# A bidirectional RWKV scan under dense products on one core: product order tied to the emission model, transposes for token rows, merged DMA issues

## The chip, the cores and the metric

One core of a Trainium2 chip. The metric is the device time of one execution in microseconds (us), from a profile of that core; lower is better. "Before" is the kernel as it stands, and the change is one edit of it.

## What is computed

One layer of a backbone over 1024 latent and 128 context tokens, D = 1024, all in float32. The part that the change touches is the token mixer:

```
h = rmsnorm(x) * (1 + scale) + shift
z = h @ w_in                       # r, k, v, low-rank decay/iclr/gate inputs, conv inputs, merge gates
for d in (forward, backward):      # 16 heads of 64
    s = s * w_t + (s @ a_t) b_t^T + v_t k_t^T ;  y_t = s @ r_t
o_a = (groupnorm(y_f + y_b) + bonus) * g
merged = g_a * (o_a @ w_pa) + g_b * (o_b @ w_pb)
x = x + gate * (merged @ w_o)      # then rmsnorm, up projection, 3-tap convolution, silu, down projection
```

The outputs are both token streams and the final scan states of the context.

## The kernel before, in words

**Dense products.** The T = 1152 token columns are cut into three stretches of 384 (`TH`). Every weight block and every input is split into a rounded high part and a rest (`split_w`, L212), so that one 128x128x384 product is three fp32r matmuls: psd<-h,whi twice and psd<-h,wlo once. A job is 128 output channels: 8 k x 3 stretches x 3 = 72 matmuls, plus evacuations on ACT or DVE. w_in has 67 jobs (4824 matmuls) and w_pb 8 (576); these 5400 run beside the scan. Then come w_pa and w_o (576 each) and the feed-forward part.

**The scan** (class `Scan`, `start` L1019) is cut into 36 items: 4 groups of four heads times 9 positions (8 latent chunks of 2 x 64 tokens for each direction, and one context item). `prep` (L1106) computes per channel pair p and stretch the decayed r, k, kk and b rows from the loads krk<-ks, kks, rs (L1114) and llo<-lo (`lora_in`, L1183) and stores them to DRAM in FA and FB (L1178). Then each item goes through: `features` (L1190: loads BK<-fb, E and O<-fa); the 64 gram products gpb, gpk (L1223) with their masks on DVE (G, E, O); `to_blocks` and `chain_load` (Dd<-G, Dm<-Dd through DRAM); `chain` (L1301), 31 x 2 dependent DVE operations Xt<-X,Dm and X<-X,Xt, whose result goes through DRAM back into G (Xd<-X on ACT's queue, G<-Xd on SP's); `merge` (L1325), a DVE transpose RSt<-G (L1330) and two rounds of 16 small products mps; bps (L1244), the token rows of b and k as products of 64x64 blocks with the identity; `vfill` (L1252), which loads v rows into Wt; and `scan` (L1356), twice per item (c = 0, 1): px<-Wt,E/O and py, copy SX, px<-SX,G, copies into Wt (ACT, and DVE COPY at L1387), px<-Wt,BT and py<-G,Wt, then two DVE adds that make the next state in Wt. `finish` (L1429) normalises the outputs (products fps) and stores them to oa, from which w_pa's inputs are loaded (x<-oa).

**Order.** Each of these is a generator, a stream. `drive` (L172) runs a model clock: `mm` adds a product's price to it, `Stream.use` books time on DVE, ACT and POOL. Between two dense matmuls, `step_streams` (L151) advances every stream whose own model time has come; what a stream emits gets a scheduling priority 20000 places ahead (`later`, `AHEAD`). The framework's scheduler then places each instruction on its engine's queue by priority and its own estimate; every engine runs its queue in order, and so a product that was put early is waited for with all dense matmuls behind it.

Of the kernel before, what the change touches and what calls it, by code (L numbers as in the profile page):

```python
# [15 lines left out]
P = 128  # L16
D = 1024
# [59 lines left out]
class Kern:  # L77
    def __init__(self, tc, ins, outs):
        self.tc, self.nc = tc, tc.nc
        self.ins, self.outs = ins, outs  # L80
        self.clk = Clock()
        self.streams = []
        self.events = set()
        self.split, self.split_next = "V", "G"


    def mm(self, out, lhsT, rhs, start, stop, cost):
        self.clk.now += cost
        return self.nc.tensor.matmul(out, lhsT=lhsT, rhs=rhs, start=start, stop=stop)  # L89

# [7 lines left out]
    def transp(self, out, in_, ident, cost=60):  # L98
        self.clk.now += cost
        return self.nc.tensor.transpose(out, in_, ident)  # L100

# [49 lines left out]
    def step_streams(self):  # L151
        while True:
            for s in list(self.streams):
                if s.t > self.clk.now:
                    continue
                if s.cond is not None and not s.cond():
                    continue
                if s.gate is not None and max(self.clk.backlog("V"), self.clk.backlog("A")) > s.gate:
                    continue
                s.cond = None  # L160
                try:
                    with self.later(-AHEAD - s.ahead):
                        r = next(s.gen)
                    if callable(r):
                        s.cond = r
                except StopIteration:
                    self.streams.remove(s)
                break
            else:
                return  # L170
# [171 lines left out]
def build(tc, ins, outs, dbg=None):  # L342
# [4 lines left out]
    with es:  # L347
# [9 lines left out]
        dt_ = lambda name, shape=(P, T): dr.tile(list(shape), F32, name=name, tag=name)  # L357
        RS = [dt_(f"rs{m}") for m in range(8)]
        KS = [dt_(f"ks{m}") for m in range(8)]
        KKS = [dt_(f"kks{m}") for m in range(8)]  # L360
        VS = [dt_(f"vs{m}") for m in range(8)]
        LO = [dt_(f"lo{m}") for m in range(4)]
# [3 lines left out]
        VT = [dt_(f"vt{d}", (T, D)) for d in range(2)]  # L366
        GS = [dt_(f"gs{m}") for m in range(8)]
# [142 lines left out]
        with ExitStack() as ea:  # L510
# [16 lines left out]
            K.sc = Scan(K, const, apool, par, pc, mask, ident, bones, x0, hw0, hka, oka,  # L527
                        dict(RS=RS, KS=KS, KKS=KKS, VS=VS, LO=LO, GS=GS, OA=OA, FA=FA, FB=FB, BS=BS, VT=VT))
            hx = lambda k: (H[k][0], H[k][1])
# [9 lines left out]
            def lora_evac(base, func):  # L539
                def ev(s, th, ps):  # L540
                    sl = slice(th * TH, th * TH + TH)
                    z = st.tile([P, TH], F32, name="lz", tag="st")
                    K.act(s, z, ps, func)
                    hi = st.tile([P, TH], F32R, name="lh", tag="st")
                    lo = st.tile([P, TH], F32R, name="ll", tag="st")
                    K.act(s, hi, z, AF.Copy)
                    K.tt(s, lo, z, hi.bitcast(F32), ALU.subtract)
                    for d in range(2):
                        K.dma(LO[base + d][0:64, sl], hi[64 * d:64 * d + 64, :].bitcast(F32), "lo")
                        K.dma(LO[base + d][64:128, sl], lo[64 * d:64 * d + 64, :].bitcast(F32), "lo")  # L550
                return ev

            job(T_WD, lora_evac(0, AF.Tanh))
            job(T_AD, lora_evac(2, AF.Copy))

# [9 lines left out]
            def g_evac(s, m, th, ps):  # L565
                z = st.tile([P, TH], F32, name="gz", tag="st")
                K.act(s, z, ps, AF.Copy)
                K.dma(GS[m][:, th * TH:th * TH + TH], z, "gs")
# [13 lines left out]
            def v_evac(m):  # L582

                def ev(s, th, ps):
# [8 lines left out]
                    def post(s2):  # L593
                        t0, ms = th * TH, slice(m * P, m * P + P)
                        for d, zd in enumerate((z, zr)):
                            yield
                            pv = K.psd.tile([P, 512], F32, name="vps", tag="psd")
                            for j in range(3):
                                K.transp(pv[:, j * P:j * P + P], zd[:, j * P:j * P + P], ident, cost=110)
                            s2.t = clk.now  # L600
                            zt = st.tile([P, 3, P], F32, name="vt", tag="st")
                            K.act(s2, zt, pv[:, :TH].rearrange("p (j f) -> p j f", f=P), AF.Copy)
                            for a, b, _ in latctx(th):
                                r0 = t0 + a if d == 0 or t0 + a >= TL else TL - t0 - b
                                K.dma(VT[d][r0:r0 + b - a, ms].rearrange("(j t) f -> t j f", t=P),
                                      zt[:, a // P:b // P], "vt")
                        K.events.add(("v", m, th))
# [76 lines left out]

            rkv(0)
            rkv(1)
            job(T_GD, gd_evac)
            gjobs()
# [295 lines left out]
class Scan:  # L984
# [4 lines left out]
    def __init__(self, K, const, apool, par, pc, mask, ident, bones, x0, hw0, hka, oka, dr):  # L989
# [25 lines left out]
        self.W = self.one.tile([P, 2, 4, 2, C], F32, name="Wt", tag="Wt")  # L1015
        self.y, self.PC = {}, {}
        self.NY = 4

    def start(self):  # L1019
# [4 lines left out]
        def prep_all(s):  # L1024
            yield lambda: ("kk", 0, 0) in ev and ("r", 0, 0) in ev
            self.lora_in(0, 0)
            for p in range(NPAIR):
                yield lambda: ("kk", p, 0) in ev and ("r", p, 0) in ev
                yield from self.lora_w(s, p)
                for th in (0, 2, 1):  # L1030
                    yield lambda: ("kk", p, th) in ev and ("r", p, th) in ev
                    yield from self.prep(s, p, th)
                    ev.add(("prep", p, th))

        def ready(i, what):
            pp, n = self.items[i]
            ths = {n // 3, (7 - n) // 3} if n < 8 else {2}
            return all((what, 2 * pp + q, th) in ev for q in range(2) for th in ths)

        def prep2_all(s):  # L1040
            for i, (pp, n) in enumerate(self.items):
                yield lambda: ready(i, "prep") and (i < 3 or ("scan", i - 3) in ev)
                self.features(s, i, pp, n)
                s.t = K.clk.now + 2500
                yield
# [60 lines left out]
    def prep(self, s, p, th):  # L1106
# [6 lines left out]
        krk = self.one.tile([P, 3, TH], F32, name="krk", tag="krk")  # L1113
        for j, src in enumerate((dr["KS"], dr["KKS"], dr["RS"])):  # L1114
            K.dma(krk[:, j, :], src[p][:, t0:t0 + TH], "ld")
        if pp not in self.PC:
# [5 lines left out]
        for d in range(2):  # L1122
# [52 lines left out]
            for a, b in segs:  # L1175
                g0 = t0 + a if d == 0 or t0 + a >= TL else TL - t0 - b
                K.act(s, PC[:, q, d, g0 // C:(g0 + b - a) // C], e65[:, a // C:b // C, C], AF.Copy)
                for dst, src in (("FA", FAo), ("FB", B)):  # L1178
                    K.dma(dr[dst][pp][:, q, d, 2 * g0:2 * (g0 + b - a)],
                          src[:, a // C:b // C].rearrange("p c a t -> p (c a t)"), "fa")  # L1180
            yield

    def lora_in(self, th, d):  # L1183

        llo = self.one.tile([P, 2, TH], F32R, name="llo", tag="llo")
        for w in range(2):
            self.K.dma(llo[:, w, :].bitcast(F32), self.dr["LO"][2 * w + d][:, th * TH:th * TH + TH], "llo")
        self.llo = llo, self.K.clk.now + 4000
# [19 lines left out]
    def prep2(self, s, i, pp, n):  # L1208
# [5 lines left out]
        for q in range(2):  # L1214
# [4 lines left out]
            for e in range(4 * q, 4 * q + 4):  # L1219
                for ps, a in ((gb, 1), (gk, 0)):  # L1220
                    for h in range(2):
                        o = HS[h if a else 1 - h]
                        calls.append(lambda ps=ps, a=a, h=h, e=e, o=o: K.mm(  # L1223
                            ps[o, e - 4 * q, :], BK[HS[h], e, a, :], (E, O)[h][HS[h], e, :], True, True, 85))
            K.group(calls)
# [12 lines left out]
        for x in range(4):  # L1238
            for c in range(2):
# [12 lines left out]
    def vfill(self, s, i, pp, n):  # L1252
# [5 lines left out]
        for c in range(2):  # L1258
# [8 lines left out]
            ch = (2 * n + c if n < 8 else c) * C  # L1267
            for d in range(2):
                rows = self.dr["VT"][d][base + ch:base + ch + C, 256 * pp:256 * pp + 256]
                rows = rows.rearrange("t (q h f) -> t q h f", q=2, h=2)  # L1270
                for h in range(2):
                    K.dma(Wt[64 - 64 * h:128 - 64 * h, h, d::2, c, :], rows[:, :, h, :], "v")
            if c == 0 and n == 8:
# [155 lines left out]
    def finish(self, s, pp, key):  # L1429
# [7 lines left out]
        for q in range(2):  # L1437
# [9 lines left out]
            v, g, b = flat(v3), flat(g3), flat(b3)  # L1447
            s.t = K.clk.now + 2500
            yield
# [83 lines left out]
```

## Time and profile before

| | us |
|---|---|
| three runs, median (lowest to highest) | 3005.72 (3000.78 to 3016.42) |
| the profiled execution | 2994.76 |
| its span | 2993.0 |
| PE busy in it | 2771.6 (93%) |
| DVE busy | 2009.7 (67%) |
| ACT busy | 1266.4 (42%) |
| mean granted TensorE clock | 0.972 of 2.4 GHz |

The profiled execution lies 0.36% under the median. A matmul's duration in the profile runs from its issue to its modelled end, and matmuls overlap, so that PE's busy time is more than the time it needs: the pitch from one dense matmul to the next is read from long pieces of the chain of waits instead.

### The profile page before, as it was taken

To read this page: it belongs to the slowest core of one execution; us is meant where nothing else is said; L and a number is where in the kernel's file an instruction comes from. 1 tells how busy PE (TensorE), PEld (TensorE's weight loads), DVE (VectorE), ACT (ScalarE), POOL (GpSimd) and SP (SyncE) were. 2 spreads that over 40 slices of the span, in tenths; PEclk is the share of its full clock that TensorE was granted. 3 is DMA by queue.
4 is the path that set the end of the run, shared out by engine and by line. 5 is a ranking of instruction groups with operands and counts; after the bars stand their busy time and mean duration, and the time that the engine had idled before them with its cause. 6 is when DMAs were issued, how large, how long until landed. Compare 5 with 4: busy or idle time off the path is not lost. (4 is left out here: it accounts for less than half of the span.)

```text
span 2993.0 us, 63336 instructions
## 1 busy us (share of the span) xinstructions
PE 2771.6 (93%) x24762; PEld 2514.2 (84%) x24762; DVE 2009.7 (67%) x5039; ACT 1266.4 (42%) x2540; POOL 318.9 (11%) x342
## 2 busy tenths in 40 slices
PE   7886989999989988988998999899999999999997
PEld 3774778878778877777777789899999999999996
DVE  8367666677568779989877865965555454454556
ACT  5464536454545633334543544023443241424243
POOL 3211111111111111111111112100000000000001
PEclk9997999999999999999999999999999999999999
DMA  4577646464655644544554538853211111111112
GB/s 191 179 240 204 197 121 209 145 180 143 184 172 166 197 118 127 136 115 122 148 136 120 137 101 279 291 165 98 68 43 36 50 40 45 41 41 43 41 44 81
DMA packets 425937, 388.50 MB, mean 130 GB/s; under 512 B 189477, under 2 KB 362405, under 8 KB 425637
## 3 DMA queue, kind: packets, MB, share of 16 engines
q1 hardware_dynamic: 379558, 360.84, 39.6%
q0 software_dynamic: 6912, 18.88, 2.3%
q10 hardware_dynamic: 39168, 4.73, 1.0%
q8 instruction: 195, 3.19, 0.5%
q14 instruction: 104, 0.85, 0.1%
HBM read 268.17 MB, written 116.13 MB: 128 GB/s over the span
## 5 line engine op out<-in xcount | busy, mean ns | idle before, releaser
L89 PE MATMUL psd<-h,whi 128*128 128x384 f32 x3216 | 909.3, 355 | 20.4 <-ACT h L105 9.3
L89 PEld LDWEIGHTS psd<-h,whi 128*128 128x128 f32 x3216 | 592.3, 192 | 58.6 <-issue 12.6
L89 PE MATMUL psd<-h,wlo 128*128 128x384 f32 x1608 | 564.5, 352 | 3.6 <-POOL wlo L110 3.6
L89 PE MATMUL psd<-g,whi 128*128 128x384 f32 (+1 forms) x2112 | 543.2, 338 | 0.0
L105 ACT ACTIVATE whi<-wraw 128x512 fp32r<-128x512 f32 (+2 forms) x334 | 198.4, 595 | 457.5 <-PE psd L89 358.6
L89 PEld LDWEIGHTS psd<-g,whi 128*128 128x128 f32 x2112 | 383.5, 188 | 0.3
L89 PE MATMUL psd<-g,wlo 128*128 128x384 f32 (+1 forms) x1056 | 355.9, 337 | 0.0
L110 POOL TENSOR_TENSOR wlo<-wraw,whi 128x512 fp32r<-128x512 f32 x148 | 207.1, 1402 | 1208.6 <-ACT whi L105 1057.4
L89 PEld LDWEIGHTS psd<-h,wlo 128*128 128x128 f32 x1608 | 309.3, 192 | 17.3 <-POOL wlo L110 5.2
L110 DVE TENSOR_TENSOR X<-X,Xt 128x60 f32<-128x60 f32 (+24 forms) x1116 | 258.0, 233 | 27.3
L110 DVE TENSOR_TENSOR Xt<-X,Dm 128x60 f32<-128x60 f32 (+24 forms) x1116 | 257.4, 233 | 27.0
L89 PE MATMUL psd<-a,whi 128*128 128x384 f32 x864 | 219.0, 334 | 0.0
L89 PE MATMUL psd<-x,whi 128*128 128x384 f32 x768 | 199.7, 341 | 8.0 <-ACT x L105 4.4
L89 PEld LDWEIGHTS psd<-g,wlo 128*128 128x128 f32 x1056 | 199.3, 189 | 0.0
L110 DVE TENSOR_TENSOR wlo<-wraw,whi 128x512 fp32r<-128x512 f32 (+2 forms) x186 | 113.7, 612 | 102.9 <-ACT whi L105 102.9
L89 PEld LDWEIGHTS psd<-a,whi 128*128 128x128 f32 x864 | 156.0, 188 | 0.0
L110 DVE TENSOR_TENSOR fu<-psd,rs 128x384 f32<-128x384 f32 x132 | 73.4, 556 | 117.3 <-PE psd L89 105.2
L89 PEld LDWEIGHTS psd<-x,whi 128*128 128x128 f32 x768 | 140.6, 191 | 10.3 <-ACT x L105 4.7
L89 PE MATMUL psd<-a,wlo 128*128 128x384 f32 x432 | 144.0, 334 | 0.0
L122 DVE SCALAR_TENSOR_TENSOR x<-psd,mod,x 128x384 f32<-128x384 f32 (+3 forms) x160 | 79.2, 515 | 93.9 <-PE psd L89 93.8
L105 ACT ACTIVATE BK<-BK,PC 128x128 f32<-128x128 f32 x288 | 93.2, 392 | 102.2 <-PE gpk L89 77.9
L89 PE MATMUL psd<-x,wlo 128*128 128x384 f32 x384 | 130.5, 340 | 5.4 <-DVE wlo L110 5.4
(206 smaller groups left out, 4917.7 us busy)
## 6 DMA issues: line engine op xcount, KB each, us to landing
wraw<-in_w_in SPq DMA_DIRECT2D x134, 256.0 KB, 3.2
wraw<-in_w_up SPq DMA_DIRECT2D x88, 256.0 KB, 2.6
llo<-lo SPq DMA_DIRECT2D x98, 192.0 KB, 2.7
BK<-fb SPq DMA_DIRECT2D x36, 512.0 KB, 4.8
Dm<-Dd POOLq DMA_DIRECT2D x144, 128.0 KB, 3.6
wx<-in_wmb SPq DMA_DIRECT2D x32, 512.0 KB, 5.3
fa<-fa SPq DMA_DIRECT2D x40, 384.0 KB, 2.7
fb<-ak SPq DMA_DIRECT2D x40, 384.0 KB, 3.0
```

Source lines behind the costliest of these rows:

```text
L89: return self.nc.tensor.matmul(out, lhsT=lhsT, rhs=rhs, start=start, stop=stop)
L105: self.nc.scalar.activation(out, in_, func, bias=bias, scale=scale)
L110: e.tensor_tensor(out, a, b, op)
L122: self.nc.vector.scalar_tensor_tensor(out, a, sc, b, op0, op1)
```

## The change

1. `mm` and `transp` called by a stream are wrapped in `issue_after(self.last)`, `last` being the dense matmul emitted last: on PE a scan product stays behind the dense matmul after which the model emitted it. DVE, ACT and DMA instructions are not bound.
2. bps becomes 16 transposes of a 64-partition slice into 128x64 per item, in place of 32 products (the trace counts two records per product). For that, FB holds the two rows b and k in swapped order for partitions 0 to 63; its store is three DMAs instead of one, two of them in runs of 256 bytes.
3. Fewer issues: krk in one load instead of three (48 fewer), llo in one instead of two (49 fewer), Wt<-vt two per step instead of four (144 fewer), with VT laid out for that; against them 112 more for FB.
4. The model's waits: a prep counts as readable 5000 ns after its stores, the loads of features take 5500 instead of 2500, those of finish 4500 instead of 2500. The job of the gate's low-rank input moves ahead of the second r, k, v jobs, and every second evacuation of the gate product goes to DVE.

```diff
 def mm(self, out, lhsT, rhs, start, stop, cost):
     self.clk.now += cost
-    return self.nc.tensor.matmul(out, lhsT=lhsT, rhs=rhs, start=start, stop=stop)
+    with self.behind():
+        r = self.nc.tensor.matmul(out, lhsT=lhsT, rhs=rhs, start=start, stop=stop)
+    if not self.stepping:
+        self.last = r.ins
+    return r
+
+def behind(self):
+    return self.tc.issue_after(self.last) if self.stepping and self.last is not None else nullcontext()
...
-        for j, src in enumerate((dr["KS"], dr["KKS"], dr["RS"])):
-            K.dma(krk[:, j, :], src[p][:, t0:t0 + TH], "ld")
+        K.dma(krk, dr["KR"][p][:, :, t0:t0 + TH], "ld")
...
-                for dst, src in (("FA", FAo), ("FB", B)):
-                    K.dma(dr[dst][pp][:, q, d, 2 * g0:2 * (g0 + b - a)],
-                          src[:, a // C:b // C].rearrange("p c a t -> p (c a t)"), "fa")
+                K.dma(dr["FA"][pp][:, q, d, cols], FAo[:, a // C:b // C].rearrange("p c a t -> p (c a t)"), "fa")
+                K.dma(dr["FB"][pp][64:128, q, d, cols], B[64:128, a // C:b // C].rearrange("p c a t -> p (c a t)"), "fb")
+                for j in range(2):
+                    K.dma(dr["FB"][pp][0:64, q, d, cols].rearrange("p (c a t) -> p c a t", a=2, t=C)[:, :, j, :],
+                          B[0:64, a // C:b // C, 1 - j, :], "fb")
...
-                s.t = K.clk.now + 2500
+                s.t = K.clk.now + 5500
...
-        K.group([lambda e=e, a=a, h=h: K.mm(pv[h][HS[h if a else 1 - h], e, :], BK[HS[h], e, a, :],
-                                            self.ident[HS[h], HS[h]], True, True, 45)
-                 for e in range(8)[::-1] for a in range(2) for h in range(2)])
+        K.group([lambda e=e, h=h: K.transp(pv[h][:, e, :], BK[HS[h], e].rearrange("p a t -> p (a t)"),
+                                           self.ident[HS[h], HS[h]], cost=40)
+                 for e in range(8)[::-1] for h in range(2)])
...
-                    K.dma(Wt[64 - 64 * h:128 - 64 * h, h, d::2, c, :], rows[:, :, h, :], "v")
+            for h in range(2):
+                K.dma(Wt[64 - 64 * h:128 - 64 * h, h, :, c, :], self.dr["VT"][base + ch:base + ch + C, pp, h], "v")
```

How many of the 5400 dense matmuls stand on PE's queue ahead of the last product of an item's scan, counted over the whole order:

| item | 0 | 11 | 24 | 35 (last) |
|---|---|---|---|---|
| before | 806 | 3114 | 3886 | 4670 |
| change | 1116 | 3401 | 5344 | 5400 |

How many stand between px<-SX,G and the px<-Wt,BT that waits for its result, in the mean of two steps an item:

| items | 1 to 11 | 12 to 24 | 25 to 35 |
|---|---|---|---|
| before | 5.2 | 3.5 | 5.3 |
| change | 11.0 | 7.1 | 0 |

PE late in the scan (psd: dense; mps: merge; bps: token rows; px, py: scan). Before, around item 25:

```order
L89 MATMUL mps<-G,RSt 32x32 x15
L89 MATMUL bps<-ident,BK 64x64 x22
L89 MATMUL px<-SX,G 64x64 x8
L89 MATMUL bps<-ident,BK 64x64 x10
L89 MATMUL psd<-h_424,whi 128x384
L89 MATMUL psd<-h_423,wlo 128x384
L89 MATMUL px<-Wt,BT 64x64 x8
L89 MATMUL py<-G,Wt 64x64 x8
```

The change, around item 33:

```order
L91 MATMUL mps<-RSt,G 32x32 x16
L91 MATMUL mps<-G,RSt 32x32 x16
L110 MATMUL bps<-ident,BK 128x64 x12
L91 MATMUL px<-SX,G 64x64 x8
L110 MATMUL bps<-ident,BK 128x64 x4
L91 MATMUL px<-Wt,BT 64x64 x8
L91 MATMUL py<-G,Wt 64x64 x8
```

From item 25 on no dense matmul stands between the products of the change.

PE at the end of the scan (fps: finish; psd<-h: w_in and w_pb; psd<-x: w_pa). Before:

```order
L89 MATMUL py<-G,Wt 64x64 x8
L89 MATMUL psd<-h_425,wlo 128x384
L89 MATMUL psd<-h_427,whi 128x384
L89 MATMUL psd<-h_428,whi 128x384
L89 MATMUL psd<-h_427,wlo 128x384
L89 MATMUL psd<-h_429,whi 128x384
L89 MATMUL psd<-h_430,whi 128x384
L89 MATMUL fps<-y,bones 128x128
```

The change:

```order
L91 MATMUL py<-G,Wt 64x64 x8
L91 MATMUL fps<-y,bones 128x128
L91 MATMUL fps<-fb,rb 128x128
L91 MATMUL fps<-fb,bones 128x128
L91 MATMUL fps<-y,bones 128x128
L91 MATMUL fps<-fb,rb 128x128
L91 MATMUL fps<-fb,bones 128x128
L91 MATMUL psd<-x_22595,whi 128x384 x3
```

Before, 730 dense matmuls (the last of w_in and all of w_pb) follow the scan; with the change w_pa's first matmul follows the last fps directly.

DVE ahead of the transpose RSt of item 16 (X, Xt: chain steps, from 128x31 for the first to 128x8 for the last; y, fv, fps, fb, rb: finish; cct: convolution). Before:

```order
L110 TENSOR_TENSOR Xt<-X,Dm 128x3x21
L116 TENSOR_SCALAR rb<-bones,par 128x128
L110 TENSOR_TENSOR X<-X,Xt 128x3x21
L110 TENSOR_TENSOR cct<-cct,psd 128x384
L110 TENSOR_TENSOR fps<-fps,fb 128x256
L110 TENSOR_TENSOR Xt<-X,Dm 128x3x20
L122 SCALAR_TENSOR_TENSOR fps<-fps,fb 128x256
L110 TENSOR_TENSOR X<-X,Xt 128x3x20
L122 SCALAR_TENSOR_TENSOR fb<-fps,fb 128x256
L1330 STREAM_TRANSPOSE RSt<-G 128x256
```

The change:

```order
L120 TENSOR_TENSOR Xt<-X,Dm 128x8
L120 TENSOR_TENSOR X<-X,Xt 128x8
L132 SCALAR_TENSOR_TENSOR y<-fps,y 128x256
L120 TENSOR_TENSOR fv<-fv,fps 128x256
L126 TENSOR_SCALAR rb<-bones,par 128x128
L120 TENSOR_TENSOR fps<-fps,fb 128x256
L132 SCALAR_TENSOR_TENSOR fps<-fps,fb 128x256
L120 TENSOR_TENSOR Xt<-X,Dm 128x31
L132 SCALAR_TENSOR_TENSOR fb<-fps,fb 128x256
L120 TENSOR_TENSOR X<-X,Xt 128x31
L1349 STREAM_TRANSPOSE RSt<-G 128x256
```

Before, item 16's chain ended some 25 rows ahead of its RSt, with steps of item 17's chain between; RSt of item 16 stands behind both Wt copies of item 15. With the change item 16's last chain step (X 128x8) is nine rows ahead of its RSt, and both Wt copies of item 15 stand behind that RSt. So it is for items 11 to 24; from item 26 on the order is again that of before.

## Rows read from the trace of the kernel before

**Rows 1.** Windows by stage: PE, PEld, DVE, ACT, POOL busy (instructions), clock, DMA share, GB/s.

```profile
233.00:342.00 109.00, 79.89 (x788) 62.75 (x790) 80.75 (x251) 49.74 (x112) 15.90 (x19) 0.81 0.64 190
342.00:1081.00 739.00, 677.07 (x6553) 595.21 (x6550) 504.97 (x1280) 372.45 (x808) 112.88 (x110) 0.96 0.56 169
1081.00:1787.00 706.00, 649.47 (x9907) 545.18 (x9907) 595.44 (x2130) 292.79 (x656) 99.98 (x137) 0.99 0.48 125
```

**Rows 2.** Windows, ACT's copies SX alone, two per item: the items of a stage.

```profile
342.00:1081.00 739.00, 8.42 (x22) 0.96 0.56 169
1081.00:1787.00 706.00, 18.47 (x48) 0.99 0.48 125
```

**Rows 3.** Chain of waits, one long piece of dense matmuls: start, us, what.

```profile
1936.00 193.99 PE psd L89 x1105
```

**Rows 4.** Chain of waits from 1780 us: the last scan step, finish, the first load for w_pa.

```profile
1784.29 0.68 PE px L89 x16
...
1786.23 0.62 PE px L89 x16
1786.85 0.61 PE py L89 x16
...
1797.80 0.34 PE fps L89 x2
...
1808.32 5.97 DMA x<-oa
...
1822.27 26.71 PE psd L89 x141
```

**Rows 5.** Timeline of PE: an item's gram products, first and last, then merge and bps.

```profile
1270.65 0.32 PE L89 MATMUL gpb<-O,BK 64*64 64x128 f32 x1
...
1273.34 0.27 PE L89 MATMUL gpk<-O,BK 64*64 64x128 f32 x1
...
1276.22 0.69 PE L89 MATMUL mps<-RSt,G 32*32 32x32 f32 x32
...
1278.71 0.99 PE L89 MATMUL bps<-ident,BK 64*64 64x64 f32 x22
...
1280.41 0.63 PE L89 MATMUL bps<-ident,BK 64*64 64x64 f32 x28
```

**Rows 6.** Timeline of PE: three transposes vps of 128x128.

```profile
1043.26 0.49 PE L100 MATMUL vps<-ident,vz 128*128 128x128 f32 x3
```

**Rows 7.** Lines of DVE, 1081 to 1787 us: busy us, mean ns, idle ahead of it.

```profile
L1387 DVE COPY Wt<-px 64x256 f32<-64x256 f32 x48 | 20.5, 428 | 39.0 <-ACT Wt L105 38.4
```

**Rows 8.** Timeline of DVE: item 20's last chain step, and its transpose RSt.

```profile
1317.49 0.18 DVE L110 TENSOR_TENSOR X<-X,Xt 128x8 f32<-128x8 f32 x1
...
1329.65 0.43 DVE L1330 STREAM_TRANSPOSE RSt<-G 128x256 f32<-128x256 f32 x1
```

**Rows 9.** DMA issues: KB each, median us from issue to landing.

```profile
BK<-fb SPq DMA_DIRECT2D x36, 512.0 KB, 4.8
...
oa<-fg SPq DMA_DIRECT2D x32, 128.0 KB, 2.6
```

**Rows 10.** Timeline of SP's queue: four issues of one item.

```profile
1324.28 1.79 SPq L128 DMA_DIRECT2D G<-Xd  x4
```

**Rows 11.** Windows, 225 to 300 us, columns as in rows 1.

```profile
225.00:300.00 75.00, 47.49 (x423) 31.89 (x422) 54.85 (x188) 33.74 (x81) 8.54 (x14) 0.70 0.70 204
```

**Rows 12.** Lines of PE, 225 to 300 us: the same gram products there.

```profile
L89 PE MATMUL gpb<-O,BK 64*64 64x128 f32 x48 | 10.1, 376 | 0.0
```

**Rows 13.** Lines of PE, 1081 to 1787 us: the gram products late in the scan.

```profile
L89 PE MATMUL gpb<-O,BK 64*64 64x128 f32 x352 | 47.4, 275 | 1.3 <-DMA O<-fa 1.2
```

**Rows 14.** Lines of DVE, 1787 to 1940 us, under w_pb: the modulation sums.

```profile
L396 DVE SCALAR_TENSOR_TENSOR wx<-wx 128x1024 f32<-128x1024 f32 x51 | 70.9, 1390 | 5.9 <-DMA wx<-in_wmb 4.6
```

**Rows 15.** Timeline of PE: the first dense matmuls of w_pa.

```profile
1927.97 0.59 PE L89 MATMUL psd<-x,whi 128*128 128x384 f32 x2 [0.31 <-issue]
```

More of the change, by code (lines that the diff above doesn't have):

```diff
@@ L1 @@
-from contextlib import ExitStack, contextmanager
+from contextlib import ExitStack, contextmanager, nullcontext
 import numpy as np
@@ L83, in __init__ @@
         self.events = set()
+        self.stepping, self.last = False, None
         self.split, self.split_next = "V", "G"
@@ L99, in transp @@
         self.clk.now += cost
-        return self.nc.tensor.transpose(out, in_, ident)
+        with self.behind():
+            return self.nc.tensor.transpose(out, in_, ident)
     def act(self, s, out, in_, func, scale=1.0, bias=0.0):
@@ L161, in step_streams @@
                 try:
+                    self.stepping = True
                     with self.later(-AHEAD - s.ahead):
@@ L167, in step_streams @@
                     self.streams.remove(s)
+                finally:
+                    self.stepping = False
                 break
@@ L357, in build @@
         dt_ = lambda name, shape=(P, T): dr.tile(list(shape), F32, name=name, tag=name)
-        RS = [dt_(f"rs{m}") for m in range(8)]
-        KS = [dt_(f"ks{m}") for m in range(8)]
-        KKS = [dt_(f"kks{m}") for m in range(8)]
+        KR = [dt_(f"kr{m}", (P, 3, T)) for m in range(8)]
+        KS, KKS, RS = [[kr[:, j] for kr in KR] for j in range(3)]
         VS = [dt_(f"vs{m}") for m in range(8)]
-        LO = [dt_(f"lo{m}") for m in range(4)]
+        LO = [dt_(f"lo{d}", (P, 2, T)) for d in range(2)]
         FA = [dt_(f"fa{m}", (P, 2, 2, 2 * T)) for m in range(4)]
@@ L365, in build @@
         BS = [dt_(f"bs{m}") for m in range(8)]
-        VT = [dt_(f"vt{d}", (T, D)) for d in range(2)]
+        VT = dt_("vt", (T, 4, 2, 4, HD))
         GS = [dt_(f"gs{m}") for m in range(8)]
@@ L527, in build @@
             K.sc = Scan(K, const, apool, par, pc, mask, ident, bones, x0, hw0, hka, oka,
-                        dict(RS=RS, KS=KS, KKS=KKS, VS=VS, LO=LO, GS=GS, OA=OA, FA=FA, FB=FB, BS=BS, VT=VT))
+                        dict(KR=KR, VS=VS, LO=LO, GS=GS, OA=OA, FA=FA, FB=FB, BS=BS, VT=VT))
             hx = lambda k: (H[k][0], H[k][1])
@@ L548, in ev @@
                     for d in range(2):
-                        K.dma(LO[base + d][0:64, sl], hi[64 * d:64 * d + 64, :].bitcast(F32), "lo")
-                        K.dma(LO[base + d][64:128, sl], lo[64 * d:64 * d + 64, :].bitcast(F32), "lo")
+                        K.dma(LO[d][0:64, base, sl], hi[64 * d:64 * d + 64, :].bitcast(F32), "lo")
+                        K.dma(LO[d][64:128, base, sl], lo[64 * d:64 * d + 64, :].bitcast(F32), "lo")
                 return ev
             job(T_WD, lora_evac(0, AF.Tanh))
-            job(T_AD, lora_evac(2, AF.Copy))
+            job(T_AD, lora_evac(1, AF.Copy))
             gts = []
@@ L565, in g_evac @@
             def g_evac(s, m, th, ps):
-                z = st.tile([P, TH], F32, name="gz", tag="st")
-                K.act(s, z, ps, AF.Copy)
+                z = st.tile([P, TH], F32, name="gs", tag="st")
+                if (m + th) % 2:
+                    K.act(s, z, ps, AF.Copy)
+                else:
+                    nc.vector.tensor_copy(z, ps)
+                    s.use("V", 530)
                 K.dma(GS[m][:, th * TH:th * TH + TH], z, "gs")
@@ L593, in post @@
                     def post(s2):
-                        t0, ms = th * TH, slice(m * P, m * P + P)
+                        t0 = th * TH
                         for d, zd in enumerate((z, zr)):
@@ L604, in post @@
                                 r0 = t0 + a if d == 0 or t0 + a >= TL else TL - t0 - b
-                                K.dma(VT[d][r0:r0 + b - a, ms].rearrange("(j t) f -> t j f", t=P),
-                                      zt[:, a // P:b // P], "vt")
+                                for h in range(2):
+                                    K.dma(VT[r0:r0 + b - a, m // 2, h, 2 * (m % 2) + d].rearrange("(j t) f -> t j f", t=P),
+                                          zt[:, a // P:b // P, h * HD:h * HD + HD], "vt")
                         K.events.add(("v", m, th))
@@ L685, in build @@
             rkv(0)
+            job(T_GD, gd_evac)
             rkv(1)
-            job(T_GD, gd_evac)
             gjobs()
@@ L1015, in __init__ @@
         self.W = self.one.tile([P, 2, 4, 2, C], F32, name="Wt", tag="Wt")
-        self.y, self.PC = {}, {}
+        self.y, self.PC, self.made = {}, {}, {}
         self.NY = 4
@@ L1032, in prep_all @@
                     yield from self.prep(s, p, th)
-                    ev.add(("prep", p, th))
+                    self.made[p, th] = K.clk.now + 5000
         def ready(i, what):
@@ L1037, in ready @@
             ths = {n // 3, (7 - n) // 3} if n < 8 else {2}
-            return all((what, 2 * pp + q, th) in ev for q in range(2) for th in ths)
+            keys = [(2 * pp + q, th) for q in range(2) for th in ths]
+            if what == "prep":
+                return all(self.made.get(k, 1e12) <= K.clk.now for k in keys)
+            return all((what, *k) in ev for k in keys)
         def prep2_all(s):
@@ L1177, in prep @@
                 K.act(s, PC[:, q, d, g0 // C:(g0 + b - a) // C], e65[:, a // C:b // C, C], AF.Copy)
-                for dst, src in (("FA", FAo), ("FB", B)):
-                    K.dma(dr[dst][pp][:, q, d, 2 * g0:2 * (g0 + b - a)],
-                          src[:, a // C:b // C].rearrange("p c a t -> p (c a t)"), "fa")
+                cols = slice(2 * g0, 2 * (g0 + b - a))
+                K.dma(dr["FA"][pp][:, q, d, cols], FAo[:, a // C:b // C].rearrange("p c a t -> p (c a t)"), "fa")
[3 more added lines that the diff above has]
+                          B[0:64, a // C:b // C, 1 - j, :], "fb")
             yield
@@ L1185, in lora_in @@
         llo = self.one.tile([P, 2, TH], F32R, name="llo", tag="llo")
-        for w in range(2):
-            self.K.dma(llo[:, w, :].bitcast(F32), self.dr["LO"][2 * w + d][:, th * TH:th * TH + TH], "llo")
+        self.K.dma(llo.bitcast(F32), self.dr["LO"][d][:, :, th * TH:th * TH + TH], "llo")
         self.llo = llo, self.K.clk.now + 4000
@@ L1223, in prep2 @@
                         calls.append(lambda ps=ps, a=a, h=h, e=e, o=o: K.mm(
-                            ps[o, e - 4 * q, :], BK[HS[h], e, a, :], (E, O)[h][HS[h], e, :], True, True, 85))
+                            ps[o, e - 4 * q, :], BK[HS[h], e, a if h else 1 - a, :], (E, O)[h][HS[h], e, :], True, True, 85))
             K.group(calls)
@@ L1267, in vfill @@
             ch = (2 * n + c if n < 8 else c) * C
[L1268 to L1271, printed above, removed]
-                    K.dma(Wt[64 - 64 * h:128 - 64 * h, h, d::2, c, :], rows[:, :, h, :], "v")
+            for h in range(2):
+                K.dma(Wt[64 - 64 * h:128 - 64 * h, h, :, c, :], self.dr["VT"][base + ch:base + ch + C, pp, h], "v")
             if c == 0 and n == 8:
@@ L1447, in finish @@
             v, g, b = flat(v3), flat(g3), flat(b3)
-            s.t = K.clk.now + 2500
+            s.t = K.clk.now + 4500
             yield
```

## The prediction

> **What bounds the kernel now.** The windows by stage come first. Between 342 and 1081 us, 11 items run (22 copies SX) and between 1081 and 1787 us another 24 [rows 1, 2]: 739/11 = 67.2 us an item, then 706/24 = 29.4. The reader should not take PE's busy shares (677 of 739, 649 of 706) for its need, since matmuls overlap. The need is worked out from pitches. A dense matmul costs 193.99/1105 = 0.1756 us [rows 3]. An item's own products cost: a scan step is five groups of 16 records at 0.61 to 0.68, about 3.15, so 6.3 for both steps [rows 4]; gram 1273.61 - 1270.65 = 3.0; merge two groups of 0.69, so 1.4; bps 64 records, of which 50 took 0.99 + 0.63, so 2.1 [rows 5]. That is 12.8 us; the few fps and the changes between dense and small products are left out.
>
> With the dense matmuls from the order's table: items 1 to 11 have 2308 of them, 210 each, so PE needs 36.8 + 12.8 = 49.6 us of 67.2, and DVE is busy 505/11 = 45.9 [rows 1]. Items 12 to 35 have 1556, 65 each: PE 11.4 + 12.8 = 24.2, DVE 595/24 = 24.8, of 29.4. So early items lose **17.6 us** beyond the larger need, late ones **4.6**. In the first stage neither engine is full: waits between engines make the difference. In the second DVE and PE are level, and the chain on DVE sets the pace. That excess is what the new order can win, and what it can lose.
>
> **Part by part.** *Order of the products.* The same 5400 dense matmuls and 36 items stand on PE, distributed otherwise, so I price stages by items.
>
> Start to item 0: before, it ended at 342 us, where the first stage of 11 items begins [rows 2], with 806 dense ahead; now 1116 stand there. The extra 310 cost 54 us; PE was idle 29 of the 109 us from 233 to 342 [rows 1], and I let about 20 of that be filled (bounds 0 and 29): 377.
>
> Items 1 to 11: 2285 dense, 208 each. Need 36.5 + 12.8 - 1.1 (bps, below) = 48.2. If products stand later than their inputs, jitter no longer stops the queue. If the streams themselves are slow, nothing changes. For a gain speaks the table of gaps: between px<-SX,G and px<-Wt,BT, where the result goes through ACT or DVE, stand 11.0 dense matmuls in the mean, 5.2 before, when five of the 22 steps had one or none. The bounds are 48.2 and 48.2 + 17.6 = 65.8; I take the middle, 57.0, since much of PE's waiting is spread over loads and prep, which the order does not touch: 11 x 57.0 = 627.
>
> Items 12 to 24: 1943 dense, 149 each: need 26.2 + 11.7 = 37.9, now PE's own bound, as DVE has 24.8 plus the wait below. The nearest row for the excess is that of late items, 4.6: 42.5, so 13 x 42.5 = 552 (bounds 37.9 and 48.5, the latter with the wait below in full).
>
> Items 25 to 35 have no dense matmul beneath them. PE's 11.7 fill only part of DVE's 24.8, and the pace is that of the late items before, 29.4, less about one for evacuations of dense products that DVE no longer has here: 11 x 28.5 = 313 (bounds 25 and 35). So the scan ends at 377 + 627 + 552 + 313 = **1869**, against 1787 before.
>
> *Behind the scan.* Before, 730 dense matmuls covered the way from the last product to w_pa's input. They are gone. From the last rows: 10.7 us from the last py, 1787.46, to the end of the last fps [rows 4], oa's store 2.6 [rows 9], the load 6.0 and 8 from its landing to the first matmul that uses it [rows 4]: 27 us uncovered. From w_pa's first matmul to the end before: 2994.8 - 1928.0 = 1066.8 [rows 15]. The modulation sums, 71 us of DVE that ran under w_pb [rows 14], now share DVE with w_pa's evacuations during 100 us of PE work (576 x 0.1756): 10, between 0 and 25. Sum: 1869 + 27 + 1067 + 10 = **2973** against 2994.8 of the profiled execution.
>
> *bps.* 16 records in place of 64. Nearest prices: 32 ns each, the pitch of bps records now, or 0.49/3 = 163 ns as vps does with twice the partitions [rows 5, 6]: 0.5 to 2.6 us against 2.1. I take 1.0, so 1.1 won an item, 40 in all, and it is in the needs above; in the last 11 items DVE hides it.
>
> *Issues.* 241 fewer and 112 more on SP's queue. They matter where something waits for SP. An issue takes 1.79/4 = 0.45 us [rows 10]: 50 us more and 108 less on a queue that is mostly free. BK<-fb lands after 4.8 [rows 9] and the grams come later than that, so I take 0; were that cover gone, the range of the two is a loss of 50 and a gain of 108. *Model's waits.* They move products behind more dense matmuls, which the table of positions already holds. *Evacuations on DVE.* 12 of 384 columns, by the copy of 256 at 0.43 [rows 7] 0.65 each: 0 to 8, taken as 0, since DVE is 68% busy there [rows 1].
>
> **The rivals.** *(a) Waits nearly vanish.* For it: late products always find their inputs. Against it: the loads and prep of the early items wait as before. With a quarter of the early excess left (52.6 us an item) and 2 late (39.9): 2973 - 48 - 34 = 2891.
>
> *(b) The X round trip stands in front of the scan (slower).* Item 20's X took 12.0 us from its last chain step to RSt [rows 8], with chain steps of the next item run meanwhile. Now, for items 12 to 24, DVE has some 3 to 10 us of work there, 6 uncovered on average, and the Wt copies of the item before are queued behind it; PE's px<-Wt,BT waits for those, with every dense matmul behind it. Between px<-SX,G and px<-Wt,BT stand 7.1 dense in the mean, 1.2 us. It decides once the delay is longer than these: 13 x 6 = 78, so 3051. Against it: the copies could be late already without harm, if the scan is far behind the chain. DVE waits for ACT's Wt, not RSt, at that place now [rows 7].
>
> *(c) The clock (slower).* From 225 to 300 us, PE ran small products, 47 of 75 us busy, and the granted clock fell to 0.70 in the mean, so to its lower level of 1.2 GHz for part of it; gram products took 376 ns there and 275 late in the scan [rows 11 to 13]. In items 25 to 35 PE has 11.7 us in 28.5. If the clock is at 1.2 GHz there, both scan steps take 6.3 us more, on the path from px to Wt: 11 x 6.3 = 69, so 3042. For items 12 to 35 before, with dense between, it was 0.99. The Trainium skill, "TensorE: Matmul & The Clock Gate", Part 1, says that the throttled clock is the default and activity releases it. By that rule the sum would be that of this rival, and the early window agrees (0.70). I give it little, since DVE, not PE, has the longest work there.
>
> *(d) The early items stay as they are.* DVE and ACT have the work they had, and both stages of the two kernels hold the same 16 preps (64 products lps). If the waits are those of prep and of the way through DRAM, the excess stays 17.6: 627 becomes 724, so 3070. The change would then not do what it says: PE's order moves, its waits remain. Against it speaks the table of gaps.
>
> **How the numbers follow.** A measurement of this kernel tells about 0.5%, 15 us, from no change. The profiled execution lies 0.37% under the median, so 11 us are added: the forecast is 2985 against 3005.7, the rivals 2902, 3063, 3053 and 3081. Chances: forecast 0.41 (its own range 2950 to 3020: 0.30 faster, 0.09 same, 0.02 slower), (a) 0.19, (b) 0.20, (c) 0.08, (d) 0.12; of (b) to (d) 0.05 falls within 0.5%. So faster 0.49, same 0.14, slower 0.37. The range 2900 to 3075 leaves out about half of (a) and of (d).
>
> **What would show it.** Scan end (the last ACT copy y<-py): 1869, against 1787 now. Copies SX by window: items 1 to 11 in 627 us, 12 to 24 in 552, 25 to 35 in 313, with PE idle for more than half of the last. (b) shows as PE waits px <- DVE Wt after RSt between items 12 and 24; (c) as a clock well under 0.9 in the tail; (d) as 65 us an early item. I am wrong in the main step if the early items take over 62 us or under 53, and in the tail if it takes over 35 us an item.

## The result

The change is **4.2% slower**: 3135.2 us in the median of four runs (3126.7 to 3139.9) against 3005.4, a ratio of 1.042 (95% interval 1.039 to 1.046). The forecast was 2985, the range 2900 to 3075: direction and range were wrong. The profiled execution took 3126.7 us.

The windows of the changed kernel, ACT's copies SX alone, two per item, cut at the ends of items 0, 11, 24 and 35 (columns as in [rows 2]: clock, DMA share, GB/s):

```profile
0.00:408.00 408.00, 0.75 (x2) 0.91 0.61 185
408.00:1152.50 744.50, 8.37 (x22) 0.92 0.59 163
1152.50:1718.00 565.50, 9.96 (x26) 0.98 0.49 136
1718.00:2023.00 305.00, 8.41 (x22) 0.73 0.41 101
```

| stage, us | forecast | measured |
|---|---|---|
| start to item 0 | 377 | 408 |
| items 1 to 11 | 627 | 744.5 |
| items 12 to 24 | 552 | 565.5 |
| items 25 to 35 | 313 | 305 |
| from there to the end | 1104 | 1103.7 |
| profiled execution | 2973 | 3126.7 |

The late stages and the way to the end came out within 14 us each. The miss of 154 us lies before item 12: 31 at the start, 117 in the early items, which took 67.7 us each and not 57. Nothing of the early gain is there [rows 2].

What PE waits for up to then has changed. The waits of PE (us in total, times, longest), 0 to 1081 us before (the same line only) and the three longest from 0 to 1150 us of the change:

```profile
PE psd L89 <- ACT whi L105: 5.0, 3, 3.3
```

```profile
PE psd L91 <- ACT whi L115: 79.2, 13, 15.9
PE psd L91 <- ACT gs L115: 12.4, 4, 6.1
PE vps L110 <- ACT vzr L115: 10.9, 6, 4.3
```

The dense matmuls themselves now stand still, for rounded weights (whi). ACT, which rounds them, in turn waits for their load (wraw), before and after:

```profile
ACT whi L105 <- DMA wraw<-in_w_in: 15.0, 10, 3.9
```

```profile
ACT whi L115 <- DMA wraw<-in_w_in: 61.5, 27, 10.5
```

The tail without dense matmuls has to be read with care. PE's granted clock is 0.73 there in the mean, between its two levels of 1.2 and 2.4 GHz, against 0.99 late in the scan before [rows 1], and px<-SX,G takes 285 ns in place of 228; yet an item takes 27.7 us and not 29.4. DVE is the busiest engine, 234 of the 305 us. PE's px, py, mps, fps and bps are still a third of the chain of waits there, so what an item would take at the full clock no run shows.

### The profile page after: what moved, and what is told of

Same layout as the page of the kernel before. It is cut to its first block, busy times and chain, and to the rows that moved or that the text cites. A ratio compares the mean times of both kernels' runs of the same rounds, so it can differ in the third digit from the quotient of the medians.

```text
span 3124.9 us, 59797 instructions
## 1 busy us (share of the span) xinstructions
PE 2748.0 (88%) x23034; PEld 2510.1 (80%) x23034; DVE 2017.9 (65%) x5051; ACT 1228.9 (39%) x2509; POOL 313.4 (10%) x342
## 4 chain that ended last, share of the span: by engine, by line
PE 51%; DVE 17%; DMA 4%; ACT 3%; issue 2%; SPq 1%; ACTq 1%; POOL 0%; DVEq 0%
PE psd L91 43%; DVE Xt L120 4%; DVE X L120 4%; PE px L91 3%; PE fps L91 1%; PE mps L91 1%; PE py L91 1%; SPq L138 1%; DMA wraw<-in_w_in 1%; PE gpb L91 1%; DMA Xd<-X 1%; DVE ak L120 1%; ACTq L138 1%; DVE Mp L120 1%; DVE y L132 1%
## 5 line engine op out<-in xcount | busy, mean ns | idle before, releaser
L91 PEld LDWEIGHTS psd<-h,whi 128*128 128x128 f32 x3216 | 602.6, 196 | 128.0 <-ACT whi L115 84.1
L120 DVE TENSOR_TENSOR Xt<-X,Dm 128x60 f32<-128x60 f32 (+24 forms) x1116 | 265.4, 239 | 41.4 <-DMA Dm<-Dd 11.6
L91 PE MATMUL psd<-x,whi 128*128 128x384 f32 x768 | 207.5, 348 | 17.6 <-ACT x L115 11.0
```

Source lines behind the costliest of these rows:

```text
L91: r = self.nc.tensor.matmul(out, lhsT=lhsT, rhs=rhs, start=start, stop=stop)
L120: e.tensor_tensor(out, a, b, op)
```

## The experiments

The parts of the change were first taken apart: binding against all the rest. The runs are called e1 to e18; the kernel before was run again beside each group, at 3004 to 3007 us.

**The rest without the binding, and the binding alone.**

```diff
 def behind(self):
-    return self.tc.issue_after(self.last) if self.stepping and self.last is not None else nullcontext()
+    return nullcontext()
```

> The changed kernel without the binding of products to the dense matmul emitted last; all else stays (transposes, merged DMAs, model waits). Its order has 879 dense matmuls ahead of item 0's end, 3094 of item 11's, 4760 of the last. Theory 1 (the binding is the loss: PE's order is moved and the orders of DVE, ACT and SP are not, so their heads wait for late products): 2960 to 3010, items 1 to 11 in 700 us or less, no dense wait for whi above 15 us. Rival 2 (the rest is the loss: FB and v stores in runs of 256 bytes, longer model waits): 3080 or more. Rival 3 (the loss is the stretch of 11 items without dense matmuls alone): 2990 to 3010, items 1 to 11 unchanged at 740.

Measured (e1): 3091.2, ratio 1.029 (1.025 to 1.032). The other corner adds `behind` and its two `with` to the kernel before:

> The kernel before with the binding alone. Its order has 1023 dense matmuls ahead of item 0's end, 5328 of item 24's, none after. Theory 1: 3110 to 3170, items 1 to 11 in 730 us or more with 50 us or more of dense waits for whi; the chain of events is that of the changed kernel. Rival 2: 3000 to 3040. Rival 3: 3090 to 3140 with waits for whi as low as before, 5 us.

Measured (e2): 3053.4, 1.016 (1.012 to 1.019). So none of the three held alone: the binding costs 47 us and the rest 85 by itself, and 47 + 85 = 132 is what both cost together (130). Theory 1 was wrong on the waits for whi, which the binding alone does not have (4.5 us). Its stages were not those expected either:

```profile
361.00:1046.00 685.00, 627.75 (x6514) 564.72 (x6510) 518.51 (x1351) 356.61 (x786) 113.41 (x111) 0.97 0.60 181
1046.00:1629.70 583.70, 544.11 (x6641) 483.15 (x6636) 387.31 (x1223) 203.21 (x444) 96.04 (x108) 0.97 0.48 133
1629.70:1950.00 320.30, 211.82 (x3814) 176.60 (x3812) 241.01 (x893) 89.09 (x233) 18.73 (x40) 0.74 0.39 95
```

These are items 1 to 11, 12 to 24 and 25 to 35 of the binding alone (columns as in [rows 1]). The early items take 62.3 us instead of 67.2: there the binding **wins** 54 us. It loses more elsewhere. Item 0 ends 19 us later (361), items 12 to 35 take 904 us and not 706, since nearly all of the dense matmuls that followed the scan now stand in it, and the way behind the scan is shorter by only 104: 19 - 54 + 198 - 104 = 59 us in the profiled executions.

**The old model waits, and a looser binding,** both on the changed kernel:

```diff
-                s.t = K.clk.now + 5500
+                s.t = K.clk.now + 2500
...
-            self.last = r.ins
+            self.past.append(r.ins)
+            self.last = self.past[max(0, len(self.past) - 1 - 300)]
```

> The changed kernel with the old model waits (2500 ns for the loads of features and of finish, a prep readable at once). The order keeps the binding: 1033 dense ahead of item 0's end, 5362 of item 24's. Theory 1 and rival 3: within 25 us of the changed kernel's 3135, since the waits shift positions only. Rival 2 as far as it names the waits: 3090 or less.

Measured (e3): 3125.6 (1.040): 10 us, so the waits are not it.

> The changed kernel with products bound to the dense matmul emitted 300 before the last (52 us of dense work earlier). Its order has 884 dense ahead of item 0's end, 3099 of item 11's, 5023 of item 24's: early items stand as before, the tail without dense begins some two items later. Theory 1: products no longer hold the queues, items 1 to 11 fall to 640 to 700 us; 3050 to 3090. Rival 3: items 1 to 11 stay at 740, item 0 ends 40 us earlier and that is given back at the end; 3110 to 3140.

Measured (e4): 3179.5 (1.058), the slowest of all. Items 1 to 11 took 793 us, about what they take without the binding (788.6 in e1). Items 12 to 35 took 887 us (870.5 in the changed kernel), the last 125 or more without dense matmuls: the loosening took the early gain away and left the late loss. Both theories were off.

**Single parts undone, in the unbound kernel** (3091). Loads apart again (llo in the same way):

```diff
-        K.dma(krk, dr["KR"][p][:, :, t0:t0 + TH], "ld")
+        for j in range(3):
+            K.dma(krk[:, j, :], dr["KR"][p][:, j, t0:t0 + TH], "ld")
```

> The unbound changed kernel (3091, 85 us over before) with krk in three loads and llo in two again; the new layouts stay. In that kernel DVE waits 51 us for krk<-kr and PE 19 for llo<-lo before 1130 us. Theory A (a merged load comes as late as its latest source, and DVE and PE wait): 3020 to 3050, with less than 20 us of these waits. Theory B (the three FB stores an entry hold SP's queue): 3080 to 3100. Theory C (longer model waits put loads and products late): 3080 to 3100.

Measured (e5): 3049.0 (1.015): half of the loss returns, as theory A had it. Its sign did not come: DVE still waits 59 us for krk<-kr, and PE 12 for llo<-lo. So why separate loads help here stays open. Transposes and FB's stores undone (`bps` and the store as before the change):

> The unbound changed kernel with bps as 32 products and FB stored by one DMA in the old order of rows. Theory B: 3020 to 3050, and PE's 44 us of waits of gpb for E<-fa fall under 15. Theory A and C: 3085 to 3130, since the products cost 1 us more an item.

Measured (e6): 3011.2 (1.003, 1.002 to 1.004): 80 of the 85 us return, and gpb's wait for E falls from 43.9 to 6.3. Each of the two parts helps, but with one store the merged loads cost little. Both are issued on SP's queue, so that is the place to look.

> The unbound changed kernel with the model's old waits (2500 ns for features and finish, a prep readable at once). Theory C: 3010 to 3050. Theories A and B: 3075 to 3100.

Measured (e7): 3075.0 (1.024), 16 us. The gate's job and its evacuations:

> The unbound changed kernel with the gate's job behind the second r, k, v jobs again and all its evacuations on ACT. Theory D (the gate's job delays the first preps; item 0 ends at 399 us there, 342 before, with only 97 more dense matmuls, 17 us, ahead): item 0 ends before 365 us and the kernel gains 30 to 60: 3030 to 3060. Theories A to C: 3080 to 3100.

Measured (e8): 3085.4 (1.027), 6 us; item 0 ended at 390 us. Neither is the main part.

**Stores or transposes, issues or short runs.** Two kernels without transposes tell this: one with the swapped stores, one with three stores of whole rows.

```diff
-                for j in range(2):
-                    K.dma(dr["FB"][pp][0:64, q, d, cols].rearrange("p (c a t) -> p c a t", a=2, t=C)[:, :, j, :],
-                          B[0:64, a // C:b // C, 1 - j, :], "fb")
+                for j in range(2):
+                    hp = slice(32 * j, 32 * j + 32)
+                    K.dma(dr["FB"][pp][hp, q, d, cols], B[hp, a // C:b // C].rearrange("p c a t -> p (c a t)"), "fb")
```

> The unbound changed kernel with bps as 32 products that read the swapped rows: FB is still stored by three DMAs in the swapped order, two of them in runs of 256 bytes, and no transposes are left. The kernel with both (3091) and with neither (3011) are 80 us apart. Theory B1 (the store is the loss): 3080 to 3110. Rival (the transposes, by another order of work, are the loss): 3005 to 3030.

Measured (e9): 3108.3 (1.035): the store, not the transposes; with them the same store took 17 us less (e1).

> The same with FB in the old order of rows, stored by three DMAs as well (64, 32 and 32 partitions), but in runs as long as before: the number of issues of the changed kernel without its short runs. Theory B2 (112 more issues at about 0.45 us hold SP's queue): 3060 to 3100, like the swapped store. Theory B3 (the short runs, 36864 more packets, keep the DMA engines busy, and loads land later): 3005 to 3030.

Measured (e10): 3106.2 (1.034), 6 us above B2's range: as slow with long runs. So the short runs are not the loss; what the two kernels share is the number of issues. The same kernel with two of the three on ACT's queue (`fbx="A"` in QUEUE):

> The kernel of e10 (three whole stores, unbound, 3106) with two of the three stores on ACT's queue: the same number of issues and bytes, 112 fewer on SP's queue. If SP's in-order queue is the place: 3005 to 3040. If the stores' number costs by itself (descriptors, later landing): 3085 or more. If an issue costs wherever it stands in order, ACT's queue being full of work for PE: 3050 to 3085.

Measured (e13): 3036.7 (1.011): 70 of 95 us return, with the same bytes and the same number of stores. So **SP's queue is the place** for most of it; whether the other 25 us come from issues on ACT or from the split into three, no run separates. The issue times, from the lines of tile ak (min, median, max ns, first and last start) before, in the unbound kernel, with three whole stores, and with two of them on ACT:

```profile
L128 SPq DMA_DIRECT2D fb<-ak x56: 319/338/919, 131.8 to 1051.9; - x56
```

```profile
L138 SPq DMA_DIRECT2D fb<-ak x168: 474/605/1005, 132.8 to 1160.6; - x168
```

```profile
L138 SPq DMA_DIRECT2D fb<-ak x168: 305/486/2131, 132.3 to 1155.0; - x168
```

```profile
L138 ACTq DMA_DIRECT2D fb<-ak x112: 308/410/1818, 131.7 to 1090.1; - x112
L138 SPq DMA_DIRECT2D fb<-ak x56: 451/486/628, 131.7 to 1089.7; - x56
```

By the medians, 56 x 0.338 = 19 us became 168 x 0.605 = 102 us of SP's time, all before 1161 us, where prep runs. The second longest of gpb's waits for E in the unbound kernel shows what that does. PE stands from 699.70 to 713.25 us; SP in that time:

```profile
698.62 1.57 SPq L138 DMA_DIRECT2D vt<-vt  x3
700.46 0.33 SPq L138 DMA_DIRECT2D fa<-fa  x1
701.32 1.82 SPq L138 DMA_DIRECT2D fb<-ak  x3
705.10 0.33 SPq L138 DMA_DIRECT2D fa<-fa  x1
705.47 0.43 SPq L138 DMA_DIRECT2D vt<-vt  x1
705.95 1.02 SPq L138 DMA_DIRECT2D Dd<-G  x2
707.01 0.56 SPq L138 DMA_DIRECT2D BK<-fb  x1
707.62 0.63 SPq L138 DMA_DIRECT2D E<-fa  x1
```

```profile
713.25 0.44 PE L91 MATMUL gpb<-E,BK 64*64 64x128 f32 x1 [13.55 <-DMA E<-fa]
```

The load of E is the last in line, behind a triple fb<-ak of 1.82 us, behind stores of other streams, and behind gaps in which the queue stands still for what its next instruction needs. What comes late is mostly data that the store does not touch: in the waits of PE up to 1130 us, the unbound kernel, then three whole stores (BK, which reads FB, is among them there), then two of them on ACT:

```profile
PE gpb L91 <- DMA E<-fa: 43.9, 4, 13.9
PE lps L91 <- DMA llo<-lo: 19.4, 9, 6.6
PE fps L91 <- DMA fb<-bs: 15.6, 5, 10.8
```

```profile
PE gpb L91 <- DMA E<-fa: 23.1, 3, 9.9
PE gpb L91 <- DMA BK<-fb: 21.9, 5, 9.3
```

```profile
PE gpb L91 <- DMA E<-fa: 4.1, 3, 1.8
PE gpb L91 <- DMA BK<-fb: 3.0, 3, 1.1
```

In the bound kernel PE's order is another, and the load that comes late there is wraw. That the queue is the place was tested without the binding only.

**Transposes without a store.** On the kernel before, partitions 64 to 127 by transposes, 0 to 63 by products:

```diff
+            calls.append(lambda e=e: K.transp(pv[1][:, e, :], BK[HS[1], e].rearrange("p a t -> p (a t)"),
+                                              self.ident[HS[1], HS[1]], cost=40))
```

> The kernel before with bps of partitions 64 to 127 as 8 transposes an item, and of partitions 0 to 63 as 16 products as before: no store changes, 40 records of PE an item instead of 64. By their pitch, 0.8 us less of PE an item, 28 us in all at most. If PE's records count: 2980 to 2997. If DVE sets the pace and the products were covered: 2997 to 3012.

Measured (e11): 3016.0 (1.005, 1.003 to 1.007), outside both ranges: 24 records of PE fewer an item and 12 us more. The early stage got shorter (item 11 ended at 1055 us, before at 1081) and the late one longer (776 us for items 12 to 35, before 706), with 106 more dense matmuls in it, 19 us; the rest of that is not explained. The whole change with one store and products:

> The changed kernel with the binding, but FB stored by one DMA and bps as products: the whole change less its transposes and their store. If the losses of the binding (47 us alone) and of the store (80) add up as the four corners said: 3045 to 3075. If the store's loss is worse under the binding, or the early waits for whi come from the binding: 3075 to 3110. If late loads were what made the binding lose: 2960 to 3020, as the prediction had it.

Measured (e12): 3040.7 (1.012, 1.009 to 1.015), 4 us below the first range: nearest to losses that add up, and the forecast gain does not appear without the triple store. PE's waits for whi and ACT's for wraw, up to 1150 us, are then 16 and 21 us, not 79 and 62:

```profile
PE psd L91 <- ACT whi L115: 16.0, 6, 6.6
```

```profile
ACT whi L115 <- DMA wraw<-in_w_in: 20.7, 10, 5.9
```

**Keeping the early gain.** An item of 12 to 35 took 29.4 us with 65 dense matmuls beneath it (before) and 27.7 to 29.1 with none (the tails), so some 65 cost it little, and they should be left for it. `behind`, put into the kernel before as in e2, is limited; the first line is that of e2:

```diff
-        return self.tc.issue_after(self.last) if self.stepping and self.last is not None else nullcontext()
+        return self.tc.issue_after(self.last) if self.stepping and self.last is not None and ("scan", 11) not in self.events else nullcontext()
```

> The kernel before with the binding until the scan of item 11 has been emitted, none after. Its order has 3353 dense matmuls ahead of item 11's end and 4903 ahead of the last, so some 500 follow the scan. If the early gain of the binding is real and the tail without dense was the loss: items 1 to 11 in 670 to 700 us, items 12 to 35 near 29.4 us each, 2960 to 2990. If the early gain is only work put off (DVE work and loads that come due later): 3000 to 3030.

Measured (e14): **2926.7, ratio 0.975 (0.973 to 0.976): faster than both kernels**, by more than expected. Its stages (items 1 to 11, then 12 to 35; columns as in [rows 1]):

```profile
360.00:1046.50 686.50, 627.10 (x6580) 564.68 (x6575) 521.15 (x1361) 356.85 (x788) 113.16 (x111) 0.98 0.60 181
1046.50:1765.00 718.50, 653.47 (x9911) 548.11 (x9912) 591.84 (x2083) 303.82 (x682) 104.18 (x137) 0.98 0.51 134
```

The early items keep the 62.4 us of the binding, the late ones take 29.9, near those of before, and some 470 dense matmuls are left to cover the way to w_pa.

> The change without transposes and their store, bound until the scan of item 11, none after. By e12 and e14 together: 2960 to 3000 if the early gain is real, 3010 to 3040 if not.

Measured (e15): 2924.7 (0.975, 0.972 to 0.978), below the first range and no better than e14, so the rest without its store adds nothing that can be measured.

> The change without binding, transposes, their store and the merged loads krk and llo: what is left are the two loads of v a step, the model's waits and the gate's job. e6 with merged loads took 3011. If the merged loads cost without the store too: 2975 to 3000. If they cost only where SP's queue is crowded: 3005 to 3020.

Measured (e16): 3021.5 (1.006, 1.004 to 1.008): just above the second expectation. Without the triple store the merged loads do not cost; e6, which has them, is 10 us faster.

> As e14 (2927), bound until the scan of item 15: 4178 dense ahead of item 18's end, 5329 of the last. Items 12 to 15 take some 15 us more each and carry 84 more dense matmuls, 15 us, so the scan itself breaks even; but hardly a dense matmul is left to cover the way to w_pa (27 us) and the modulation sums (10). If that cover is what the late binding costs: 2940 to 2970. If binding later items wins as binding early ones does: 2900 to 2920.

Measured (e17): 2945.7 (0.980), within the first range. The windows of SX, up to item 11 and on to the end of the scan:

```profile
358.00:1045.00 687.00, 8.37 (x22) 0.97 0.60 180
1045.00:1835.00 790.00, 18.43 (x48) 0.98 0.50 135
```

The scan ends 70 us later than in e14, with 426 more dense matmuls in it, 75 us, so it breaks even; the way behind it gets only 44 us shorter. The cover was worth some 31 us, 37 were expected.

> As e14, bound until the scan of item 5 only. If the gain accrues item by item, 6 of 12 bound items give about half: 2955 to 2975. If it comes from the start (first items late, all later ones with their inputs ready): 2925 to 2940. If it comes from items 6 to 11 alone: 2990 or more.

Measured (e18): 2937.9 (0.978), within the second range: measured against the kernel before in the same group, 69 of the 77 us of e14 come with 6 of 12 bound items. The windows of SX:

```profile
0.00:356.70 356.70, 0.78 (x2) 0.95 0.63 204
356.70:1008.50 651.80, 8.40 (x22) 0.98 0.62 186
```

Item 5 ended at 669 us with 2114 dense matmuls done; before, it ended at 672 with 1835. So 279 more, 49 us of work, are done by then, and 242 of them already at the end of item 0 (1048 by 357 us, before 806 by 342). Items 6 to 11, no longer bound, then have 168 beneath each and not 213, and take 56.6 us and not 68.2. The runs show where the time is won; why the bound order leaves PE less idle there was argued from the table of gaps and not tested.

## Why the prediction was wrong

- **"I take 0" for the issues** is the step that failed. The loss was bounded at 50 us by 112 issues at 0.45, beside a gain of 108; both were put at nothing because the queue was "mostly free" and because the reader of the store comes later. Measured: an issue of the new stores takes 0.605, SP's time for FB grew by 83 us, and the cost was 80 to 97 us (e6, e9, e10). Between the whole change (3126.7 in the profile) and the same with one store and products (3037.0, e12) lie 90 of the 154 us. In e12 the windows of SX are

```profile
0.00:379.00 379.00, 0.75 (x2) 0.94 0.64 202
379.00:1064.60 685.60, 8.39 (x22) 0.97 0.60 176
1064.60:1626.50 561.90, 9.96 (x26) 0.98 0.49 137
1626.50:1935.00 308.50, 8.39 (x22) 0.74 0.40 99
```

  and the start stands as forecast (379 against 377). The count was wrong as well: with VT laid out anew, its stores vt<-vt became 128 where they were 64, so 176 issues were added against 241 removed. Before and after:

```profile
L128 SPq DMA_DIRECT2D vt<-vt x64: 360/427/1736, 140.0 to 1051.4; - x64
```

```profile
L138 SPq DMA_DIRECT2D vt<-vt x128: 360/474/1690, 138.9 to 1061.1; - x128
```

  No run undoes these 64 alone; e6 has them and lies 7 us above before. By median times counts, an estimate, the change adds 83 us for FB and 33 for vt on SP's queue, all of it before the end of item 11. The removed issues free 118 (krk 18, llo 14, Wt<-vt 86), but only 62 of them by then. Over the whole kernel the two cancel, and where the loss lies SP had some 54 us more.
- **The early items: the direction right, the size off.** The bound order did mean less waiting, though no run shows that the gaps are the reason. The middle between the bounds, 57.0 us an item, should have been 62.3 (e2, e12): 11 x 5.3 = 58 us, the other part of the miss. In e2 these items have 212 dense matmuls each, so PE needs 37.2 + 12.8 = 50.0, and 12.3 of the 17.6 us of excess stay.
- **Items 12 to 24** (552, measured 565.5, in e12 562), **the tail** (313; 305) and **what comes behind it** (1104; 1103.7) were right, the last by two errors that cancel: from the scan's end to w_pa's first matmul it took 21 us, not 27, and 1083 from there, not 1077.
- **Rival (b)**, the X round trip ahead of the scan: in the waits of DVE from 1152 to 1718 us, RSt waits 20 us for G<-Xd in all, where 78 was its price. It is there and small; PE's px waits 7 us there for DVE's Wt.

```profile
DVE RSt L1349 <- DMA G<-Xd: 20.4, 4, 7.0
```

- **Rival (c)**, the clock: its condition came true (0.73 in the tail), its price did not: an item took 27.7 us where the forecast without it had 28.5. The price took twice the time for both scan steps; px<-SX,G took 285 ns in place of 228. The window that it was read from (225 to 300 us) held not only small products: 48 psd<-gz of 128x384 were 26.5 of PE's 47.5 us. The rule cited there from the Trainium skill ("TensorE: Matmul & The Clock Gate", Part 1) agrees on the clock.
- **Rival (d)**, the early items as before, gives nearly the right stage (724 against 744.5 measured) for a wrong reason: without the triple store the excess does fall. That its 3081 lies nearest to 3135 is luck.
- That the order gains early and loses late was not put as one question. PE's idle time in the tail, 305 - 11 x 11.7 = 176 us, was in the sum, and so was the uncovered way. What was not asked is where the binding should stop: stopped at item 11 (e14), neither is paid.

## What to carry over

Price an added DMA issue on its queue, in the stage where it falls, and ask what stands behind it in line; do not net it against issues removed elsewhere. Where one stage has free engine time and the next can hide only some filler work, give the first what it can hide and keep the rest for the second: here 3006 became 2927. And take four corners (part, rest, both, neither) before a story: none of the three first theories came through them.

## What the runs showed that was not expected

- In the median an issue of the same store takes 0.338 us as one whole, 0.486 as one of three in long runs, and 0.605 in the swapped order with short ones; yet the kernels with short and long runs take the same time (3108 and 3106).
- Without dense matmuls the granted clock of the tail is 0.73 to 0.74, and its items take 27.7 to 29.1 us, no more than late items with dense matmuls at 0.99 (29.4).
- Fewer PE records did not mean less time: half of the transposes cost 12 us on the kernel before, and why its late items got slower is open.
